# A one-core hybrid encoder layer: instructions placed by a model of the engines' timelines

## The chip, the core and the metric

The kernel runs on one core of a Trainium2 chip. The core has five engines that run their own instruction streams in order and meet only at semaphores: PE (TensorE, matmuls, with its weight loads shown apart as PEld), DVE (VectorE), ACT (ScalarE), POOL (GpSimd) and SP (SyncE, which here issues the DMAs). The metric is the device time of one execution in microseconds, lower is better.

## What is computed

One step of an encoder layer on 512 prompt frames and 64 sample frames, width 2048:

```python
mod = silu(c) @ w_ada + b_ada                       # 6 modulation vectors
h = rmsnorm(x, norm1) * (1 + sc1) + sh1
proj = h @ w_in                                     # q, k, v, gates of two mixers
o_a = gla(...)                                      # gated linear attention, 4 heads
o_b = gated_delta_rule(conv(q), conv(k), conv(v))   # 8 heads, needs a triangular inverse
x = x + g1 * (concat(o_a, o_b) @ w_out)
h = rmsnorm(x, norm2) * (1 + sc2) + sh2
x = x + g2 * (silu(causal_conv(h @ w_gate) + b) * (h @ w_val)) @ w_down
y = rmsnorm(x, final_norm)
```

The gated delta rule works in blocks. For one block it is, in short:

```python
lower = strict_tril((k * beta) @ k.T * decay)
sol = solve(eye + lower, [v * beta, k * beta * exp(G)])
u = sol_v - sol_k @ s
o = (q * exp(G)) @ s + (q @ k.T * decay) @ u
s = exp(G_last) * s + (k * exp(G_last - G)).T @ u
```

Both recurrences also return their states, and so do the two convolutions.

## The kernel before

Every product with a large weight is written as three float32r matmuls on split operands. A weight tile of 128 x 1024 is loaded by SP, ACT rounds it into a high part `wh` (L599) and DVE subtracts to get the low part `wl` (L600); PE then runs `wh` on the high and the low half of the activations (L512) and `wl` on the high half (L514). Three buffers each hold `raw`, `wh` and `wl`. The results lie in the two PSUM buffers named `g`. "Weight product" below means these L512 and L514 matmuls.

The stages stand in this order on PE. The head (0 to about 225 us of the profiled execution) loads x, transposes it (L645), makes the first modulation with matmuls at L672, and does the first products. Then the input projection runs tile by tile, while the recurrences are written as Python generators called jobs: after every six weight matmuls `tick` calls `job_step`, which advances the oldest job by one `yield`. It also advances the modulation blocks that DVE sums up (L772) and PE reduces (L778). The output projection of the second half of the heads follows, then that of the first half (about 1300 us), then the up projection as a seven-product scheme (L1300 to L1302, up to about 2400 us), then the down projection with the final norm (L1510).

The job of the gated delta rule (`gdn`, L155) runs once for each of the eight heads and a ninth time for the samples. Its steps on PE: transposes of k and q (L144, through `transpose4`), `kn.T kn` (L216), `kn.T q` (L222), then an inverse of the 16 x 16 diagonal blocks off PE (`inverse16`), then L238 and L244 twice with a transpose behind each pair, L253 and L258, the transposes of v, and four blocks of the recurrence itself, each of them a chain L276, L283, L289, with L303 and L305 for the output. Between any two of these stands a short operation of DVE or ACT that reads the PSUM bank and writes the next operand. At the end stands a norm (ACT squares, POOL power at L138, ACT scaling) and a transpose.

`inverse16` (L331) leaves PE altogether: the block goes to DRAM (L340), comes back transposed by four DMAs (L345), POOL runs 14 pairs of L351 and L352 on it, and it goes out and in again (L355, L358) before DVE spreads it (L362) for L238. `yield WAIT` and the numbers `REST_D` and `REST_X` make the job pass its turn some times while this runs.

What sets the order on each engine is the scheduler of the framework. It takes the instructions as traced, each with a priority (program order, moved forward by `high_priority(offset=80)` for the job's DVE and ACT operations and for the loading and splitting of weights), plays them on a model of the machine, and lays down for each engine the order in which they started there. Buffers limit it: the jobs and the gates of the linear attention (`gla_gate`, L1009) share 14 buffers `m` and 6 buffers `qkv`, and a tile that finds none free waits for a release.

## Time and profile before

| quantity | value |
|---|---|
| time, median of 3 runs | 2975.83 us (2970.51 to 2976.37) |
| profiled execution | 2988.47 us |
| its span, first to last instruction | 2986.8 us |
| PE busy | 2871.2 us (96%) |
| DVE busy | 2048.5 us (69%) |
| ACT busy | 1198.7 us (40%) |
| POOL busy | 334.5 us (11%) |
| HBM traffic | 131 GB/s over the span |
| mean granted clock of PE | 0.978 |

The profiled execution is 12.6 us longer than the median of the runs. In the page's slices PE is at nine tenths or more from the second tenth of the span on; in the windows that the prediction quotes it stands idle for a few per cent before 1300 us and hardly at all between 1300 and 2900 us. In those windows the columns are the busy time of each engine with its number of instructions, then the granted clock of PE (1.00 is full), the share of time in which the DMA engines were busy, and GB/s.

### The profile page before, as it was taken

The page shows a single profiled execution, that of the slowest core. Times are in us where ns is not written, and L with a number is a line of the kernel's source. Part 1 is how long each engine was busy: PE and PEld are TensorE (multiplying, and loading weights), DVE is VectorE, ACT ScalarE, POOL GpSimd, SP SyncE. Part 2 cuts the span into 40 slices and gives each one's busy share as a digit, 9 for nine tenths or more (in the row PEclk, how much of TensorE's full clock was granted, in tenths as well). Part 3 has the DMA queues.
Part 4 walks back from the last instruction along what each step waited for, and adds up shares of the span by engine and source line. Part 5 has one row for each costly group of instructions (what it writes and reads, how often), then busy time and mean ns, then how long its engine had stood idle before and what let it go on. Part 6 is the DMA issues. An engine that isn't in the chain of part 4 may idle for free.

```text
span 2986.8 us, 52415 instructions
## 1 busy us (share of the span) xinstructions
PE 2871.2 (96%) x21096; PEld 2774.8 (93%) x21096; DVE 2048.5 (69%) x3198; ACT 1198.7 (40%) x2062; POOL 334.5 (11%) x609
## 2 busy tenths in 40 slices
PE   6998899999899999999999999999999999999998
PEld 3688889999799998999999999999999999999997
DVE  2355776667568867557888888888888865555555
ACT  4235454444435433245444444444444421222223
POOL 0004342232210000000011011111101100000000
PEclk7999999999899999999999999999999999999999
DMA  8964554445454446743333333333333473333221
GB/s 251 286 191 118 143 161 130 129 129 147 123 156 131 140 128 184 201 141 97 111 104 105 113 100 106 113 104 104 114 106 104 133 235 101 111 101 115 86 80 65
DMA packets 535446, 395.55 MB, mean 132 GB/s; under 512 B 59657, under 2 KB 465412, under 8 KB 535204
## 3 DMA queue, kind: packets, MB, share of 16 engines
q1 hardware_dynamic: 535204, 392.21, 44.7%
q8 instruction: 166, 2.72, 0.4%
q14 instruction: 76, 0.62, 0.1%
HBM read 356.47 MB, written 35.67 MB: 131 GB/s over the span
## 4 chain that ended last, share of the span: by engine, by line
PE 80%; DVE 6%; DMA 4%; POOL 4%; ACT 3%; issue 2%; SPq 0%; ACTq 0%; POOLq 0%; DVEq 0%
PE g L512 25%; PE g L514 13%; PE bank L1301 11%; PE bank L1300 11%; PE bank L1302 11%; DVE acc L772 2%; DMA xr<-in_w_ada_dram 1%; PE bank L144 1%; PE bank L672 1%; POOL m L352 1%; POOL m L351 1%; POOL s L138 1%; PE bank L405 1%; PE bank L778 1%; ACT m L1623 1%
## 5 line engine op out<-in xcount | busy, mean ns | idle before, releaser
L1301 PE MATMUL bank<-slot,wh 128*128 128x290 f32 x2464 | 736.2, 299 | 0.0
L1300 PE MATMUL bank<-slot,wh 128*128 128x290 f32 x2464 | 733.9, 298 | 0.0
L1302 PE MATMUL bank<-slot,wl 128*128 128x290 f32 x2464 | 728.0, 295 | 0.0
L512 PE MATMUL g<-slot,wh 128*128 128x288 f32 x3168 | 551.6, 295 | 0.2 <-DVE slot L1070 0.2
L512 PE MATMUL g<-hh,wh 128*128 128x288 f32 x2048 | 470.0, 308 | 2.4 <-ACT wh L599 2.4
L1302 PEld LDWEIGHTS bank<-slot,wl 128*128 128x128 f32 x2464 | 470.6, 191 | 0.0
L1301 PEld LDWEIGHTS bank<-slot,wh 128*128 128x128 f32 x2464 | 469.7, 191 | 0.1
L512 PEld LDWEIGHTS g<-slot,wh 128*128 128x128 f32 x3168 | 465.8, 188 | 0.7 <-DVE slot L1070 0.5
L1300 PEld LDWEIGHTS bank<-slot,wh 128*128 128x128 f32 x2464 | 464.1, 188 | 0.1
L514 PE MATMUL g<-hh,wl 128*128 128x288 f32 x2048 | 461.9, 304 | 1.2 <-DVE wl L600 1.2
L599 ACT ACTIVATE wh<-raw 128x1024 fp32r<-128x1024 f32 x215 | 227.2, 1058 | 586.6 <-PE g L512 571.4
L512 PE MATMUL g<-hl,wh 128*128 128x288 f32 x2048 | 460.6, 304 | 0.0
L1070 DVE SCALAR_TENSOR_TENSOR slot<-g,mod,slot 128x512 f32<-128x512 f32 (+1 forms) x448 | 201.9, 491 | 287.9 <-PE g L514 286.3
L772 DVE SCALAR_TENSOR_TENSOR acc<-xr,ct,acc 128x512 f32<-128x512 f32 x480 | 341.5, 754 | 29.0 <-DMA xr<-in_w_ada_dram 28.1
L512 PEld LDWEIGHTS g<-hh,wh 128*128 128x128 f32 x2048 | 337.7, 193 | 14.7 <-issue 10.2
L514 PEld LDWEIGHTS g<-hh,wl 128*128 128x128 f32 x2048 | 338.9, 193 | 8.3 <-issue 6.0
L514 PE MATMUL g<-slot,wl 128*128 128x288 f32 x1584 | 342.8, 295 | 0.0
L512 PEld LDWEIGHTS g<-hl,wh 128*128 128x128 f32 x2048 | 338.9, 193 | 4.1 <-issue 3.7
L600 DVE TENSOR_TENSOR wl<-raw,wh 128x1024 fp32r<-128x1024 f32 x215 | 262.0, 1219 | 64.9 <-ACT wh L599 63.3
L1247 ACT ACTIVATE wh<-raw 128x1024 fp32r<-128x1024 f32 x176 | 186.0, 1057 | 222.6 <-PE bank L1301 194.2
L514 PEld LDWEIGHTS g<-slot,wl 128*128 128x128 f32 x1584 | 255.3, 188 | 0.0
L1248 DVE TENSOR_TENSOR wl<-raw,wh 128x1024 fp32r<-128x1024 f32 x176 | 215.4, 1224 | 54.0 <-ACT wh L1247 54.0
(346 smaller groups left out, 3180.4 us busy)
## 6 DMA issues: line engine op xcount, KB each, us to landing
raw<-in_w_up_dram SPq DMA_DIRECT2D x176, 512.0 KB
xr<-in_w_ada_dram SPq DMA_DIRECT2D x128, 512.0 KB
raw<-in_w_in_dram SPq DMA_DIRECT2D x100, 512.0 KB
raw<-in_w_down_dram SPq DMA_DIRECT2D x88, 512.0 KB
hraw<-in_w_ada_dram SPq DMA_DIRECT2D x64, 512.0 KB
raw<-in_w_out_dram SPq DMA_DIRECT2D x32, 512.0 KB
slot<-actd SPq DMA_DIRECT2D x44, 288.0 KB
actd<-v SPq DMA_DIRECT2D x44, 256.0 KB
```

Source lines behind the costliest of these rows:

```text
L138: self.nc.gpsimd.tensor_tensor(out[:parts, :n], out[:parts, :n], self.mhalf[:parts, :n], op=ALU.pow)
L512: T.matmul(ps[:, h if bank is None else bank, :n], wh, x[:, h, :n], start=f, stop=False)
L514: T.matmul(ps[:, h if bank is None else bank, :n], wl, ah[:, h, :n], start=False, stop=stop)
L599: nc.scalar.activation(hi[:, :n_], raw[:, :n_], AF.Copy)
L600: nc.vector.tensor_tensor(lo[:, :n_], raw[:, :n_], hi[:, :n_].bitcast(F32), op=ALU.subtract)
L772: V.scalar_tensor_tensor(acc[s], w[:, k], col, acc[s], op0=ALU.mult, op1=ALU.add)
L1070: self.nc.vector.scalar_tensor_tensor(x1[:, :, z], ps[:, :, c], gain[:, q:q + 1], x1[:, :, z], op0=ALU.mult, op1=ALU.add)
L1247: self.nc.scalar.activation(hi, src, AF.Copy)
L1248: self.nc.vector.tensor_tensor(lo, src, hi.bitcast(F32), op=ALU.subtract)
L1300: T.matmul(ps, wh[:, j], hi, start=(c < 3 and j == 0), stop=False, skip_group_check=True)
L1301: T.matmul(ps, wh[:, j], lo, start=False, stop=False, skip_group_check=True)
L1302: T.matmul(ps, wl[:, j], hi, start=False, stop=(j == NPAIR - 1), skip_group_check=True)
```

## The change

One argument is added where the context of the framework is opened. The traced instructions, their priorities, the tiles and the number of buffers stay as they are. What changes is the model on which the scheduler plays them: it keeps timelines for the engines in place of the plain one.

```diff
-    with tile.TileContext(nc) as tc:
+    with tile.TileContext(nc, schedule_with_timeline_sim=True) as tc:
         layer_kernel(tc, i, o)
```

Each engine has as many instructions as before (20165 on PE, 3200 on DVE, 1894 on ACT, 614 on POOL, 1138 on SP) in another order. From the up projection to the middle of the down projection the orders are nearly alike. They differ most between the third weight tile of the projections and the end of the recurrences. Three places on PE follow. The names in the rows: `g` is the output of a weight product, `bank` of any other matmul, `wh` and `wl` the weights, `hh` and `hl` the activations, `st`, `sq`, `m` and `qkv` the operands of a job.

The first is in the recurrence of the fourth head, at 518.9 us of the profiled execution. Before:

```order
L289 MATMUL bank_759_5241<-sq_758_5233,m_595_4109 128x128
L303 MATMUL bank_761_5245<-sq_758_5233,m_590_4077 128x128
L305 MATMUL bank_761_5245<-st_752_5206,qkv_561_3883 128x128
L512 MATMUL g_742_5163<-hl_206_1231,wh_767_5272 128x288
L276 MATMUL bank_762_5256<-st_760_5243,m_612_4266 128x128
L514 MATMUL g_742_5163<-hh_205_1230,wl_768_5273 128x288 x2
L512 MATMUL g_742_5163<-hh_244_1495,wh_767_5272 128x288 x2
L283 MATMUL bank_764_5266<-sq_763_5257,m_691_4768 128x128
```

The same step in the changed kernel:

```order
L305 MATMUL bank_761_5245<-st_752_5206,qkv_561_3883 128x128
L514 MATMUL g_1023_7039<-hh_152_915,wl_1026_7042 128x288 x2
L512 MATMUL g_1023_7039<-hh_191_1180,wh_1030_7115 128x288 x2
L512 MATMUL g_1023_7039<-hl_192_1181,wh_1030_7115 128x288 x2
L514 MATMUL g_1023_7039<-hh_191_1180,wl_1031_7116 128x288 x2
L512 MATMUL g_1023_7039<-hh_195_1192,wh_1030_7115 128x288 x2
L512 MATMUL g_1023_7039<-hl_196_1193,wh_1030_7115 128x288 x2
L514 MATMUL g_1023_7039<-hh_195_1192,wl_1031_7116 128x288 x2
L512 MATMUL g_1023_7039<-hh_200_1211,wh_1030_7115 128x288 x2
L512 MATMUL g_1023_7039<-hl_201_1212,wh_1030_7115 128x288 x2
L514 MATMUL g_1023_7039<-hh_200_1211,wl_1031_7116 128x288 x2
L276 MATMUL bank_762_5256<-st_760_5243,m_612_4266 128x128
```

Between L305 and L276 stood one weight matmul and now stand twenty, and they belong to a weight product that came several tiles later before (`g_1023` in place of `g_742`): the job runs later against the products.

The second is in the recurrence of the seventh head, at 745 us of the profiled execution. Before:

```order
L276 MATMUL bank_1109_7702<-st_1106_7688,m_964_6742 128x128
L512 MATMUL g_1096_7645<-hl_245_1496,wh_1121_7754 128x288 x2
L514 MATMUL g_1096_7645<-hh_244_1495,wl_1122_7755 128x288 x2
L512 MATMUL g_1096_7645<-hh_247_1506,wh_1121_7754 128x288 x2
L283 MATMUL bank_1111_7712<-sq_1110_7703,m_1043_7244 128x128
L512 MATMUL g_1096_7645<-hl_248_1507,wh_1121_7754 128x288 x2
L514 MATMUL g_1096_7645<-hh_247_1506,wl_1122_7755 128x288
L289 MATMUL bank_1113_7723<-sq_1112_7714,m_947_6585 128x128
L303 MATMUL bank_1115_7727<-sq_1112_7714,m_942_6553 128x128
```

The same steps in the changed kernel:

```order
L276 MATMUL bank_1109_7702<-st_1106_7688,m_964_6742 128x128
L283 MATMUL bank_1111_7712<-sq_1110_7703,m_1043_7244 128x128
L289 MATMUL bank_1113_7723<-sq_1112_7714,m_947_6585 128x128
L303 MATMUL bank_1115_7727<-sq_1112_7714,m_942_6553 128x128
L305 MATMUL bank_1115_7727<-st_1106_7688,qkv_915_6364 128x128
L276 MATMUL bank_1116_7738<-st_1114_7725,m_964_6742 128x128
L283 MATMUL bank_1118_7748<-sq_1117_7739,m_1043_7244 128x128
L289 MATMUL bank_1123_7765<-sq_1119_7750,m_947_6585 128x128
L303 MATMUL bank_1125_7769<-sq_1119_7750,m_942_6553 128x128
```

Here the weight matmuls between the links are gone: the weight tiles of the last head's projections stand ahead of this place now, and the next one (`g_1273`) comes 34 rows after this L276. From the middle of the sixth head's recurrence to that tile, 83 rows, there is no weight matmul at all.

The third is around the first L238 of the samples' recurrence, at 876 us. Before:

```order
L512 MATMUL g_1312_9062<-hh_94_581,wh_1314_9064 128x288 x2
L512 MATMUL g_1312_9062<-hl_95_582,wh_1314_9064 128x288 x2
L514 MATMUL g_1312_9062<-hh_94_581,wl_1315_9065 128x288 x2
L238 MATMUL bank_1317_9090<-m_1291_8919,m_1263_8658 128x64 x4
L512 MATMUL g_1312_9062<-hh_99_600,wh_1314_9064 128x288 x2
L512 MATMUL g_1312_9062<-hl_100_601,wh_1314_9064 128x288 x2
L514 MATMUL g_1312_9062<-hh_99_600,wl_1315_9065 128x288 x2
L512 MATMUL g_1312_9062<-hh_138_865,wh_1314_9064 128x288 x2
```

In the changed kernel:

```order
L1009 MATMUL bank_1307_9039<-na_1766,wg_1848 128x512
L1009 MATMUL bank_1308_9050<-na_1766,wg_1848 128x64
L238 MATMUL bank_1317_9090<-m_1291_8919,m_1263_8658 128x64 x4
L244 MATMUL bank_1318_9102<-m_1190_8232,m_1290_8918 128x64 x4
L144 MATMUL bank_1319_9115<-consts0_96,m_1291_8919 128x128 x4
L238 MATMUL bank_1320_9128<-m_1291_8919,m_1263_8658 128x64 x4
L244 MATMUL bank_1321_9140<-m_1190_8232,m_1290_8918 128x64 x4
L144 MATMUL bank_1323_9155<-consts0_96,qkv_1322_9153 128x128 x4
L276 MATMUL bank_1332_9185<-s0_1330_9181,m_1261_8640 64x128
L276 MATMUL bank_1332_9185<-s0_1331_9183,m_1261_8640 64x128
L283 MATMUL bank_1334_9196<-sq_1333_9186,m_1291_8919 128x128
L512 MATMUL g_1410_9579<-hh_85_550,wh_1412_9581 128x288 x2
```

Between this L238 and the L216 from which its inverse starts stood 130 rows before, most of them weight matmuls. Now stand there L222 x4, L144 x4, eight matmuls of L778 and the two of L1009, and no weight matmul.

## The prediction

> **What bounds the kernel now.** I read the page first: its span, the busy times, the slices and the chain.
>
> ```profile
> span 2986.8 us, 52415 instructions
> ...
> PE 2871.2 (96%) x21096; PEld 2774.8 (93%) x21096; DVE 2048.5 (69%) x3198; ACT 1198.7 (40%) x2062; POOL 334.5 (11%) x609
> ...
> PE   6998899999899999999999999999999999999998
> ...
> PEclk7999999999899999999999999999999999999999
> ...
> PE 80%; DVE 6%; DMA 4%; POOL 4%; ACT 3%; issue 2%; SPq 0%; ACTq 0%; POOLq 0%; DVEq 0%
> ```
>
> PE is the bound, and 80% of the chain is its own work. The order of instructions cannot make that work smaller; it can only change the time in which PE stands or runs at a lower clock. So the second view is the busy time by stage (us, busy PE, PEld, DVE, ACT, POOL with counts, clock, DMA share, GB/s):
>
> ```profile
> 0.00:225.00 225.00, 190.48 (x1225) 139.29 (x1226) 94.69 (x211) 73.53 (x130) 9.00 (x25) 0.92 0.79 242
> 225.00:660.00 435.00, 402.32 (x2977) 388.61 (x2976) 289.20 (x468) 219.31 (x559) 140.87 (x283) 0.95 0.49 136
> 660.00:925.00 265.00, 246.23 (x1817) 233.75 (x1815) 174.89 (x304) 118.49 (x289) 57.00 (x120) 0.95 0.50 141
> 925.00:1300.00 375.00, 361.76 (x2610) 345.89 (x2609) 265.58 (x485) 137.28 (x241) 11.13 (x25) 0.99 0.56 158
> 1300.00:1400.00 100.00, 100.00 (x759) 100.00 (x759) 69.15 (x126) 55.36 (x102) 4.81 (x17) 1.00 0.36 109
> 1400.00:2900.00 1500.00, 1497.41 (x11170) 1496.74 (x11169) 1105.18 (x1482) 567.61 (x677) 108.11 (x134) 1.00 0.38 112
> ```
>
> From 1300 to 2900 us PE loses 2.6 us in all and has its full clock; there the change can gain nothing, and the orders are nearly alike. At 759 matmuls in 100 us a weight matmul takes 0.132 us, which is my rate for work put between two job steps. What can be won lies ahead of 1300 us. I count loss as idle time plus (1 - clock) x length, an upper measure, since part of the low clock falls into idle time: 225 to 660 us loses 32.7 + 21.8 = 54, 660 to 925 us loses 18.8 + 13.3 = 32, 925 to 1300 us 13.2 + 3.8 = 17. The head loses 34.5 + 18 = 52, but there the DMA engines are 79% busy.
>
> What PE waits for in those stretches (who, releaser, us, times, longest; three stretches in turn):
>
> ```profile
> PE bank L144 <- ACT m L1623: 20.3, 7, 6.4
> PE bank L276 <- DVE st L1623: 6.1, 1, 6.1
> PE bank L144 <- ACT qkv L924: 3.9, 2, 2.4
> ...
> PE bank L144 <- ACT m L1623: 13.1, 6, 10.3
> PE bank L283 <- DVE m L1623: 2.5, 1, 2.5
> ...
> PE bank L144 <- DMA xr<-in_x_prompt_dram: 3.4, 4, 1.8
> PE bank L1224 <- DVE dg L1218: 2.6, 1, 2.6
> PE g L512 <- ACT wh L599: 2.4, 1, 2.4
> ```
>
> Almost all are links of the jobs: PE has come to a job's next matmul before ACT or DVE has made its operand. Weights are late once.
>
> **The change, stage by stage.** Nothing is added or removed; every job step is moved against the weight matmuls, on PE, DVE, ACT, POOL and SP alike, the DMAs of the inverse and the modulation with them.
>
> *225 to 660 us, the first heads.* What one step of the recurrence takes is in the instructions of PE and DVE in order of time:
>
> ```profile
> 517.00 0.49 PE L276 MATMUL bank<-st,m 128*128 128x128 f32 x2
> ...
> 518.00 0.49 PE L283 MATMUL bank<-sq,m 128*128 128x128 f32 x2
> ...
> 518.86 0.49 PE L289 MATMUL bank<-sq,m 128*128 128x128 f32 x2
> 519.18 0.39 PE L303 MATMUL bank<-sq,m 128*128 128x128 f32 x2
> 519.40 0.39 PE L305 MATMUL bank<-st,qkv 128*128 128x128 f32 x2
> ...
> 519.78 0.49 PE L276 MATMUL bank<-st,m 128*128 128x128 f32 x2
> ```
>
> A link takes 0.86 to 1.0 us and the step 2.78 us, of which the five job matmuls are 1.1 (five at 0.22, the distance from L303 to L305). Counted over the 36 links that end at L283, the middle one had 0.8 us of PE work to cover it and has 3.05 now, as the first place shown has: twenty weight matmuls, 2.6 us, where one stood. A link of 1 us is hidden then, with 2 us to spare for an ACT or DVE that is busy with something else. Waits of 6 us are not hidden whole. I leave 10 us of the idle time, from 3 (no link but the longest late) to 20 (the waits of L144 stay, since its cause is a queue and not the distance). The clock follows the waits:
>
> ```profile
> 386.00:393.00 7.00, 3.78 (x16) 3.77 (x17) 0.69 (x1) 1.97 (x5) 2.43 (x6) 0.55 0.61 138
> 567.00:574.00 7.00, 7.00 (x36) 7.00 (x35) 3.59 (x8) 3.98 (x20) 2.46 (x3) 0.54 0.71 208
> 642.00:649.00 7.00, 7.00 (x38) 6.98 (x36) 0.92 (x3) 3.89 (x19) 1.01 (x1) 0.55 0.29 76
> 758.00:772.00 14.00, 5.67 (x24) 5.66 (x25) 7.00 (x12) 1.97 (x5) 1.68 (x2) 0.53 0.68 186
> ...
> PE bank L144 <- ACT qkv L924: 1.5, 1, 1.5
> ```
>
> The last row is from the list of waits just ahead of the 642 us row: 1.5 us were enough for 7 us at about half clock with PE fully busy. So I take 8 of the 21.8 us as staying, with bounds 3 and 18. Gain: 54 - 18 = 36, between 54 - 38 = 16 and 54 - 6 = 48.
>
> [...]
>
> *660 to 925 us, the last heads.* The jobs now run later against the products, so the products come to their end with more than two heads' steps still to do, and the next tile waits for the buffers that those jobs hold. The second and third places shown are there. These stretches have the bare links:
>
> Of the L283 links 11 have under 0.6 us of cover now, where none had. I count 9 whole steps without cover: 9 x (2.78 - 1.1) = 15. Three norms at the end of a head now have their transpose right behind L305, with 0.14 us of work between. The link took this long before:
>
> ```profile
> 677.85 0.39 PE L305 MATMUL bank<-st,qkv 128*128 128x128 f32 x2
> ...
> 681.53 0.33 PE L144 MATMUL bank<-consts,m 128*128 128x128 f32 x1 [0.91 <-ACT m L1623]
> ```
>
> That is 3.7 us, so 3 x 3.7 = 11. The second half of the inverse, L238 to L258, without cover for the seventh head and half of it for the eighth and the samples: 10 links x 0.75 = 7. And the first half, off PE, at 839 us, of all engines in order of time, with the wait ahead of an instruction in brackets:
>
> ```profile
> 839.39 1.13 PE L216 MATMUL bank<-m 128*128 128x128 f32 x8
> ...
> 841.56 0.34 SPq L340 DMA_DIRECT2D d<-m  x1
> ...
> 845.85 1.40 SPq L345 DMA_DIRECT2D m<-d  x4
> ...
> 848.68 0.12 POOL L347 MEMSET m<- 32x16 f32 x1 [13.86 <-DMA m<-d]
> ...
> 860.59 0.32 SPq L355 DMA_DIRECT2D d<-m  x1
> ...
> 863.94 0.92 SPq L358 DMA_DIRECT2D cm<-d  x2
> ...
> 865.86 1.29 DVE L362 TENSOR_TENSOR m<-cm,consts 128x512 f32<-128x512 f32 x2 [6.06 <-DMA cm<-d]
> ```
>
> From L216 to the end of L362 pass 27.8 us. L238 needs that. In the samples' job the changed order puts 5 us of PE work between them (L222 and L144, eight of L778, two of L1009), so PE stands for 23. In the eighth head it puts 9 us, but the seventh head's recurrence and norm lie in between and wait for about 12 us of the terms above, so 7 are left. Sum 15 + 11 + 7 + 23 + 7 = 63, and 11 for clock and for waits that stay: 74 against 32 before, a loss of 42. Bounds: if a quarter of the links turn out covered and nothing else waits, 0.75 x 33 + 30 = 55, a loss of 23; if the low clock covers the whole stretch, with its 27 us of job matmuls at half rate, 101, a loss of 69.
>
> *925 to 1410 us.* The transposes of x (L144 and L1099) stand 4 to 6 us of PE work later against the products than before, which covers waits up to 1.8 us, and L1224 stands 3.2 us later, which covers its 2.6. The linear attention's links get 3 us as well; at some places a transpose or an eviction on ACT now stands close ahead of a product. With the low clock at the norm 23 us are lost there before; I leave 12. Gain 11, between 3 and 16.
>
> *Head and end.* In the head transposes and modulation matmuls change places, but the transfers that set it are the same: gain 3, between -5 and 6. The last transposes (L1510) stand closer behind their residuals, with 1.6 to 2.2 us of products between; the end is the same chain: 0.
>
> *Sum.* -36 + 42 - 11 - 3 = -8. The profiled execution took 2988.47 us, its span and 1.7 around it, so it would be 2980; the median of the runs is 12.6 below it, and 2975.8 - 8 = 2968.
>
> **Rivals.**
>
> *The stretch without products runs at half clock* (slower). Its place is between the sixth head's recurrence and `g_1273`, and the samples' inverse. The 758 us row speaks for it: 14 us at 0.53 with PE 40% busy. Against it: before that, in the same head, PE was dense with job matmuls and products mixed. Then the late stages lose 101 rather than 74, the sum is +19, and the time 2995. The change is slower from a late loss of 82 us on (32 + 36 + 11 + 3).
>
> *Both sides turn out at their good end* (faster). The early waits go with their clock (48), the late links have a quarter covered (+23), and the attention gains 16: -48 + 23 - 16 = -41, or 2935. For it speak the 3 us of cover; against it that 6 us waits came from DVE and ACT being held by other work, which the order does not cure.
>
> *The waits of the first heads stay* (slower). L144 waits for a chain through ACT and POOL which are as busy as before, and an eviction of `g` on ACT behind a job's operation can hold a product. The early gain is then 16 and the sum +12: 2988. Against it: the L276 and L283 links are simple, and their cover is three times what they take.
>
> **How the numbers follow.** The forecast has 0.45, half clock late 0.22, both good 0.20, waits that stay 0.13. From run to run the kernel before agrees to 0.2%, so 6 us on either side of 2975.8 are no difference. The forecast's own range is 2953 to 2984: 0.25 of it is faster, 0.14 the same, 0.06 slower. With both good, faster is 0.45; the same is 0.14 + 0.02 of the rest, 0.16; slower 0.39. The range goes from 2935, the good rival, to 3008, half clock late with 13 more, most of what the head (8) and the attention (8) can fall short.
>
> **What would show it.** Right: between 225 and 660 us a clock of 0.98 or more and PE idle for about 10 us; L238 in the list of PE's waits with one of about 20 us; a window of some 60 us with PE at half. Wrong: L144's waits for ACT unchanged in the first heads; L238 without a long wait, which would mean that the inverse starts earlier than L216's place says; a wait of a product for `wh`, `wl` or a bank of `g` among the longest.

## The result and the profile after

The changed kernel takes 3096.91 us (median of 4 runs, 3093.65 to 3097.89), the kernel before 2976.10 us in the same set (4 runs, 2970.51 to 2980.33). The ratio is 1.0396, with a 95% interval of 1.038 to 1.0413: 121 us slower. The forecast was 2968, its range ended at 3008.

The page of the changed kernel, its span, busy times, slices of PE and of the clock:

```profile
span 3095.1 us, 52436 instructions
...
PE 2891.1 (93%) x21096; PEld 2810.2 (91%) x21096; DVE 2046.5 (66%) x3198; ACT 1199.5 (39%) x2062; POOL 296.5 (10%) x609
...
PE   6999999988595899899999999999999999999998
...
PEclk8999999998586899899999999999999999999999
```

The hole lies between the ninth and the fourteenth slice, about 600 to 1070 us. Before it, the slices are fuller than they were.

To see where the time went, the two kernels must be compared at the same work, not at the same time. I gave each matmul the median distance from one start to the next that its line has in the trace of before, and summed that along PE's order: "PE work". The time at which a place is reached, less the PE work ahead of it, is what has been lost so far. Idle time is what the records show between matmuls; the rest of a loss is matmuls that ran slowly (in the head it comes out negative, since the median distances hold some idle time of their own). The head's figures hang on the price given to the L672 matmuls, whose starts come in bunches; the other stages hardly move with it.

| PE work, us | before: lost (idle + slow) | changed: lost (idle + slow) | forecast difference | measured |
|---|---|---|---|---|
| 0 to 200, head | 29.0 (30.7 - 1.7) | 20.0 (34.0 - 13.9) | -3 | -9 |
| 200 to 550, first heads | 59.1 (32.7 + 26.4) | 25.0 (13.7 + 11.2) | -36 | -34 |
| 550 to 800, last heads | 40.1 (18.8 + 21.4) | 166.4 (106.9 + 59.4) | +42 | +126 |
| 800 to 1100, linear attention | 31.8 (13.2 + 18.5) | 55.7 (26.7 + 29.0) | -11 | +24 |
| 1100 to 2600 | 5.9 | 10.7 | 0 | +5 |

The sum is +112; the spans differ by 108. The same stages as windows, first of before, then of the changed kernel (length, busy PE, PEld, DVE, ACT, POOL with counts, clock, DMA share, GB/s):

```profile
232.00:642.00 410.00, 377.32 (x2800) 364.32 (x2799) 277.15 (x446) 204.97 (x515) 136.59 (x277) 0.96 0.50 139
642.00:932.00 290.00, 271.23 (x1996) 258.04 (x1995) 186.62 (x334) 129.57 (x321) 59.54 (x123) 0.95 0.47 131
932.00:1263.00 331.00, 317.76 (x2285) 302.82 (x2284) 243.08 (x445) 121.07 (x215) 11.13 (x25) 0.99 0.57 162
```

```profile
225.00:598.00 373.00, 359.27 (x2740) 356.57 (x2740) 222.63 (x347) 168.32 (x403) 108.86 (x233) 0.97 0.45 128
598.00:1015.00 417.00, 310.07 (x2028) 291.90 (x2027) 220.96 (x381) 157.16 (x416) 80.12 (x167) 0.77 0.40 116
1015.00:1370.00 355.00, 328.28 (x2296) 313.82 (x2294) 257.85 (x491) 126.93 (x227) 10.02 (x25) 0.93 0.51 147
```

About the same number of matmuls took 373 us in place of 410, then 417 in place of 290, then 355 in place of 331. What PE waited for in the middle stretch of the changed kernel (who, releaser, us, times, longest):

```profile
PE bank L144 <- ACT m L1623: 37.8, 4, 11.9
PE bank L238 <- DVE m L362: 30.0, 1, 30.0
PE bank L283 <- DVE sq L1623: 10.3, 9, 2.6
PE bank L289 <- ACT sq L1623: 6.3, 11, 1.0
PE bank L144 <- DVE m L1623: 5.6, 3, 3.2
PE bank L276 <- DVE st L1623: 5.4, 4, 2.1
```

The 30.0 of L238 is the samples' inverse, for which I had 23. The 37.8 are four norms, at the ends of the fourth to the seventh head, 8 to 12 us each; I had three, at 3.7. The last of them, from the end of the seventh head's recurrence to its transpose, in order of time:

```profile
838.12 0.63 PE L305 MATMUL bank<-st,qkv 128*128 128x128 f32 x2
...
839.40 0.19 ACT L1623 ACTIVATION_READ_ACCUMULATOR sq<-m 128x1 f32 x1
...
842.14 0.75 DVE L772 SCALAR_TENSOR_TENSOR acc<-xr,ct,acc 128x512 f32<-128x512 f32 x1 [4.96 <-DMA xr<-in_w_ada_dram]
842.88 0.69 DVE L362 TENSOR_TENSOR m<-cm,consts 128x512 f32<-128x512 f32 x1
843.49 0.74 DVE L772 SCALAR_TENSOR_TENSOR acc<-xr,ct,acc 128x512 f32<-128x512 f32 x1
844.15 0.68 DVE L362 TENSOR_TENSOR m<-cm,consts 128x512 f32<-128x512 f32 x1
844.75 0.34 DVE L1623 SCALAR_TENSOR_TENSOR st<-st,egl,bank 128x128 f32<-128x128 f32 x1
845.01 1.41 DVE L772 SCALAR_TENSOR_TENSOR acc<-xr,ct,acc 128x512 f32<-128x512 f32 x2
...
846.34 0.16 DVE L137 TENSOR_SCALAR s<-s 128x4 f32<-128x4 f32 x1
846.58 1.01 POOL L138 TENSOR_TENSOR s<-s,mhalf 128x4 f32<-128x4 f32 x1 [8.67 <-DVE s L137]
847.62 1.28 ACT L1623 ACTIVATE m<-m,s 128x128 f32<-128x128 f32 x4 [8.03 <-POOL s L138]
848.07 0.18 PEld L144 LDWEIGHTS bank<-consts,m 128*128 128x128 f32 x1 [9.62 <-ACT m L1623]
```

ACT has the sums of squares at 839.6. L137, which needs nothing else, starts at 846.3. In between DVE stands for 5 us in front of a sum of the modulation (L772), whose transfer has not landed, and then does four sums and three other operations that stand ahead of L137 in its order. The norm, and PE behind it, wait for a transfer that has nothing to do with them. The list of waits names ACT, two steps from the cause.

In the other three norms ACT itself is the larger part. The longest, at the end of the fourth head:

```profile
614.07 0.63 PE L305 MATMUL bank<-st,qkv 128*128 128x128 f32 x2
614.48 1.28 ACT L1623 ACT_TABLE_LOAD   x1
...
616.95 1.28 ACT L924 ACT_TABLE_LOAD   x1
...
618.89 1.28 ACT L1623 ACT_TABLE_LOAD   x1
...
623.57 0.19 ACT L1623 ACTIVATION_READ_ACCUMULATOR sq<-m 128x1 f32 x1
624.30 0.16 DVE L137 TENSOR_SCALAR s<-s 128x4 f32<-128x4 f32 x1
...
626.60 0.48 PE L144 MATMUL bank<-consts,m 128*128 128x128 f32 x1 [11.90 <-ACT m L1623]
```

Here the squares are ready only at 623.8 us, since ACT does operations of the heads to come and three table loads of 1.28 us between them; the step to DVE adds 0.5 us. At the ends of the fourth, fifth and sixth head the squares are ready 9.7, 9.7 and 5.7 us after L305 starts, at the seventh 1.5 us, and in the kernel before 1.2 or 1.3 us at every head.

### The profile page after: what moved, and what is told of

Its sections match the earlier page's. It is cut to its first block, busy times and chain, and to the rows that moved or that the text cites. A ratio compares the mean times of both kernels' runs of the same rounds, so it can differ in the third digit from the quotient of the medians.

```text
span 3095.1 us, 52436 instructions
## 1 busy us (share of the span) xinstructions
PE 2891.1 (93%) x21096; PEld 2810.2 (91%) x21096; DVE 2046.5 (66%) x3198; ACT 1199.5 (39%) x2062; POOL 296.5 (10%) x609
## 4 chain that ended last, share of the span: by engine, by line
PE 60%; DMA 2%; DVE 1%; ACT 0%; issue 0%; POOL 0%; ACTq 0%; SPq 0%; DVEq 0%; POOLq 0%
PE g L512 18%; PE bank L1301 11%; PE bank L1300 11%; PE bank L1302 10%; PE g L514 9%; DMA xr<-in_w_ada_dram 1%; DMA xr<-in_x_prompt_dram 0%; PE bank L1510 0%; DVE acc L772 0%; PE bank L144 0%; PE bank L405 0%; DVE slot L1152 0%; DMA slot<-xd 0%; PE bank L778 0%; POOL slot L1134 0%
## 5 line engine op out<-in xcount | busy, mean ns | idle before, releaser
L1302 PE MATMUL bank<-slot,wl 128*128 128x290 f32 x2464 | 714.8, 296 | 0.6 <-DVE wl L1248 0.6
L512 PE MATMUL g<-hh,wh 128*128 128x288 f32 x2048 | 461.2, 305 | 4.9 <-ACT ts L1049 1.9
L772 DVE SCALAR_TENSOR_TENSOR acc<-xr,ct,acc 128x512 f32<-128x512 f32 x480 | 338.7, 751 | 65.0 <-DMA xr<-in_w_ada_dram 64.9
L600 DVE TENSOR_TENSOR wl<-raw,wh 128x1024 fp32r<-128x1024 f32 x215 | 262.7, 1222 | 108.7 <-ACT wh L599 107.0
```

The source lines that it names most:

```text
L512: T.matmul(ps[:, h if bank is None else bank, :n], wh, x[:, h, :n], start=f, stop=False)
L600: nc.vector.tensor_tensor(lo[:, :n_], raw[:, :n_], hi[:, :n_].bitcast(F32), op=ALU.subtract)
L772: V.scalar_tensor_tensor(acc[s], w[:, k], col, acc[s], op0=ALU.mult, op1=ALU.add)
L1302: T.matmul(ps, wl[:, j], hi, start=False, stop=(j == NPAIR - 1), skip_group_check=True)
```

## The experiments

The time of the kernel before in the sets below was 2981.83 (first four), 2982.51 (next four), 2982.86 (next four) and 2980.63 us (last). Single runs are given as such. The losses by stage, worked out as above:

| kernel | us | head | first heads | last heads | attention |
|---|---|---|---|---|---|
| before (profiled 2988.47) | 2976.10 | 29 | 59 | 40 | 32 |
| changed | 3096.91 | 20 | 25 | 166 | 56 |
| e1 at most 8 steps behind | 3040.66 | 22 | 88 | 53 | 48 |
| e2 at most 32 steps behind | 3038.14 | 24 | 31 | 95 | 59 |
| e3 changed, short inverse | 3069.82 | 20 | 11 | 153 | 56 |
| e4 before, short inverse | 2938.15 | 29 | 29 | 23 | 30 |
| e5 timeline, PE of before | 3099.00 | 29 | 98 | 78 | 60 |
| e6 plain, PE of changed | 3160.26 | 33 | 63 | 190 | 44 |
| e7 before, inverse on DVE | 2960.15 | 27 | 44 | 26 | 37 |
| e8 from 32 steps to 8 | 3068.63 | 24 | 98 | 72 | 44 |
| e9 timeline, PE and DVE of before | 2997.03 | 29 | 72 | 31 | 36 |
| e10 timeline, PE and ACT of before | 3096.20 | 33 | 100 | 67 | 66 |
| e11 changed, few sums | 3031.57 | 25 | 24 | 121 | 32 |
| e12 before, few sums | 2964.41 | 31 | 49 | 23 | 33 |

**e1 and e2: how far the jobs may fall behind.** `mm6` is put under the framework's rule that its matmuls come on PE after a given instruction, here the last matmul of the job step traced `LAG` steps earlier:

```diff
+LAG = 8            # 32 in e2
...
-            self.job_step()
+            self.paced_step()      # notes the step's last PE instruction in self.steps
...
-    def mm6(self, ps, wh, wl, act, start, stop, halves=((0, HT), (1, HT)), bank=None):
+    def mm6(self, *a, **kw):
+        with self.paced():
+            self.mm6_now(*a, **kw)
...
+def _paced(self):
+    steps = getattr(self, "steps", [])
+    if not getattr(self, "jobs", None) or len(steps) <= LAG:
+        return nullcontext()
+    return self.tc.issue_after(steps[-1 - LAG])
```

> The changed kernel with one rule added: a weight matmul may not be placed on PE ahead of the last matmul of the job step that was traced eight job steps before it. So the jobs can't fall further behind the products than eight steps; the timeline model still sets the rest, DVE, ACT, POOL and SP among it. Theory 'lag' (the late loss comes from PE's products running ahead until the buffers stop them, which leaves 27 and 10 us of job matmuls bare): the gain of the first heads stays (about 40 us against before), the late loss goes, no stretch at half clock and no L238 wait over 10 us: 2920 to 2955 us. Theory 'other queues' (the timeline model's order on DVE and ACT puts the convolutions and the modulation's sums ahead of the jobs' links, and that is what PE waits for): the waits of L144 for ACT stay at 40 us or more, the time stays above 3040 us.

> The same rule with 32 job steps in place of eight. In this order 10 us of job matmuls stand bare after the seventh head and 10 us in the samples' inverse, against 27 and 10 in the changed kernel. Theory 'lag': the loss follows the bare stretch, so the time lies between the eight-step kernel and the changed one: 2990 to 3050 us, with the L238 wait of some 25 to 30 us still there, since only 4.3 us of PE work stand between L216 and L238 as in the changed kernel. Theory 'other queues': no different from the changed kernel, 3080 us or more.

Eight steps: 3040.66 us (3038.12 to 3045.88, 4 runs), ratio 1.0201, interval 1.0172 to 1.023. That is far above the range of "lag" and just on the bound of "other queues" (above 3040), whose other sign is missing: L144 waits 21.3 us for ACT, not 40 or more. The stages say why. The loss in the last heads fell from 166 to 53 us, close to the 40 of before: that part of "lag" held. But the first heads lost 88 in place of 25. With the products bound to the jobs, PE met the jobs' late links there:

```profile
PE bank L144 <- ACT m L1623: 21.2, 4, 19.5
PE bank L144 <- DVE m L1623: 17.3, 9, 4.1
PE bank L144 <- ACT qkv L924: 9.3, 2, 7.7
```

This is the list of waits of e1 from 225 to 664 us. Its PE order is near that of before (a matmul stands 8 rows away on the average, of 20165), and yet these three rows come to 47.8 us, where the same three had 25.2 in the kernel before (20.3, 1.0 and 3.9). The one wait of 19.5 us is a matter of SP: ACT stands there for a transfer of `gd` (L170) that SP issues at 264.7 us, right behind the last transfers of the inverse (L355 at 262.1, L358 at 263.8). So the links themselves have become slower with the changed kernel's orders on the other engines, and its products, running ahead, hid it in the first heads. Thirty-two steps, 3038.14 us (one run, expected 2990 to 3050): 31 us lost in the first heads and 95 in the last, with the L238 wait of 30.3 us still there. In the last heads the loss follows the bare stretch, as "lag" says; the whole time does not lie between the eight-step kernel and the changed one, as it had, since the first heads lose little here.

**e3 and e4: what the inverse costs.**

```diff
             for i in range(1, 15):
...
-            G.tensor_tensor(xt[:, rest, :i], ..., op=ALU.mult)
-            G.tensor_tensor(xx[:, rest, :i], ..., op=ALU.add)
+            if i == 1:
+                G.tensor_tensor(xt[:, rest, :i], ..., op=ALU.mult)
+                G.tensor_tensor(xx[:, rest, :i], ..., op=ALU.add)
```

> The changed kernel with one of the 14 pairs of L351 and L352 left, the other 13 left out (the inverse of the 16 x 16 blocks is not computed). The bare stretches of PE's order stay. If the samples' first inverse is exposed as I read it, L238's wait of 30 us shrinks by the pairs' time, about 11 us, to about 19, and the time falls by 11 to 16 us, to about 3083. If the wait is made by the transfers of the inverse alone or by something else ahead of L362 on DVE, wait and time stay within 4 us.

> The kernel before with the same 13 pairs left out. There the inverse has 35 to 53 us of PE work to hide behind, so nothing is won: 2968 to 2982 us. If it falls by more than 8 us, the inverse was on the path before too, and my price of its exposure in the changed kernel is too high by that.

The changed kernel took 3069.82 us (one run), 27 less; L238's wait went from 30.0 to 15.6. So the inverse is bare there, and 14 us of the 27 are that wait. I had expected 11 to 16 us in all; the rest came mostly in the first heads, which lost 11 in place of 25. The kernel before took 2938.15 us (one run), 44 less than before in the same set. That miss is a find: in the kernel before no L238 waited for the inverse, and leaving its pairs out still won 44 us. The order of time before one of the L144 waits of 6.4 us, in the trace of before, shows how:

```profile
381.08 0.19 ACT L1623 ACTIVATION_READ_ACCUMULATOR sq<-m 128x1 f32 x1
...
381.62 0.27 DVE L137 TENSOR_SCALAR s<-s 128x4 f32<-128x4 f32 x1
...
384.12 1.14 POOL L352 TENSOR_TENSOR m<-m 32x44 f32<-32x44 f32 x1
...
387.15 0.59 POOL L354 COPY m<-m 32x256 f32<-32x256 f32 x1
387.72 1.01 POOL L138 TENSOR_TENSOR s<-s,mhalf 128x4 f32<-128x4 f32 x1
...
388.76 1.28 ACT L1623 ACTIVATE m<-m,s 128x128 f32<-128x128 f32 x4 [6.55 <-POOL s L138]
389.22 0.18 PEld L144 LDWEIGHTS bank<-consts,m 128*128 128x128 f32 x1 [6.66 <-ACT m L1623]
```

L137 has its result at 381.9; L138 starts at 387.7, since POOL is in the middle of the next head's run of pairs. The norm of one head waits in POOL's queue behind the inverse of the next.

**e7: the inverse off POOL.**

```diff
-            G.tensor_tensor(xt[:, rest, :i], ..., op=ALU.mult)
-            G.tensor_tensor(xx[:, rest, :i], ..., op=ALU.add)
+            nc.vector.tensor_tensor(xt[:, rest, :i], ..., op=ALU.mult)
+            nc.vector.tensor_tensor(xx[:, rest, :i], ..., op=ALU.add)
```

> The kernel before with the 14 pairs of the inverse on DVE in place of POOL; nothing is left out. Leaving 13 of the pairs out won 44 us, though no L238 waited: POOL's 12 us run of pairs stands ahead of a norm's L138, and PE waits for that norm. If POOL's queue is the cause, the pairs on DVE win most of it, less what 28 short operations cost in DVE's queue (about 4 us a head, mostly beside other work): 2940 to 2962 us, with L144's waits for ACT under 15 us. If it is the inverse's own length that counts, or DVE is as full as POOL, 2970 to 2995 us.

2960.15 us (2956.34 to 2961.16, 4 runs), ratio to before 0.9918, interval 0.9896 to 0.994. It is the fastest kernel of this study that leaves nothing out. The waits of PE from 225 to 700 us, where L144 had waited 21.2 us for ACT in the kernel before:

```profile
PE bank L144 <- ACT m L1623: 11.2, 8, 3.4
PE g L514 <- DVE wl L600: 6.1, 1, 6.1
```

The L144 waits are halved, and a weight split on DVE is late once instead. Half of the 44 us comes back; the other half is what the pairs cost in DVE's queue, or what stays in POOL's; these runs do not part the two.

**e5 and e6: PE's order of the one, the rest of the other.** All matmuls are chained in a given order by a list of instruction numbers; the model then places the other engines round them.

```diff
-        layer_kernel(tc, i, o)
+        layer_kernel(tc, i, o); _pin(tc)
...
+def _pin(tc):                       # ORDER: the numbers of PE's instructions, in the other kernel's order
...
+    ins = {x.name: x for x in tc.nc.cur_bb.bb.instructions}
+    for ids in json.loads(zlib.decompress(base64.b85decode(ORDER))).values():
+        last = None
+        for n in ids:
+            x = ins.get(f"I-{n}")
...
+            if last is not None:
+                tc.add_manual_dep(x, last.name, mybir.DependencyInfo(mybir.DependencyClass.NoSync, mybir.DependencyReason.DATA),
+                                  reason="issue_after")
+            last = x
```

> The timeline model stays on, but PE's 20165 instructions are held to the order of the kernel before; DVE, ACT, POOL and SP are placed by the timeline model round them. Theory 'PE order': the whole difference comes from where the job matmuls stand against the products, so the kernel goes like the one before: 2965 to 2990 us, and from 550 to 800 us of PE work about 40 us are lost, as before, where the changed kernel loses 166. Theory 'other queues': the timeline's order on ACT, DVE and POOL costs by itself, so 3010 us or more.

> The mirror image: the plain model, with PE held to the changed kernel's order. Theory 'PE order': 3080 to 3110 us, with an L238 wait of about 30 us and a clock of 0.5 to 0.8 from 700 to 900 us. Theory 'other queues': the plain placing of ACT and DVE gives the links faster, the waits of L144 for ACT fall from 46 us to under 20, and the time is 3050 us or less.

The timeline model with PE's order of before: 3099.00 us (one run), as slow as the changed kernel, though every matmul stands in the order of the kernel before. "PE order" as the whole cause falls. The loss lies elsewhere than in the changed kernel, 98 in the first heads and 78 in the last. The shares of the chain that ended last, from 233 to 681 us of e5, and under it from 232 to 642 us of before:

```profile
by line: DVE acc L772 14.6%; PE g L512 11.5%; issue 7.5%; ACT m L1623 5.7%; PE g L514 5.5%; DMA xr<-in_w_ada_dram 5.2%; POOL m L352 4.9%; DVE wl L600 4.9%; POOL m L351 4.6%; DVE ca L922 4.3%; DMA d<-m 4.0%; PE bank L144 3.3%; DMA m<-gd 2.7%
```

```profile
by line: PE g L512 18.7%; PE g L514 9.4%; POOL m L352 7.2%; POOL m L351 6.7%; DVE acc L772 5.8%; issue 5.6%; ACT m L1623 4.5%; DMA xr<-in_w_ada_dram 4.4%; PE bank L144 4.2%; DVE ca L922 3.0%; POOL s L138 3.0%; DMA d<-m 2.5%; PE bank L778 1.
```

The sums of the modulation went from 5.8% of the chain to 14.6%. In e5's DVE order the jobs' operations (L1623) stand 4.6 places later than before on the average, up to 21, and L772 4.0 earlier. That is little beside PE's order, where the change moves some matmuls by hundreds of rows, and I had not looked at it.

The mirror image, plain with the changed kernel's PE order, took 3160.26 us (one run), outside both theories: three products wait 18 to 23 us for `ts` of L965 on ACT, 64 us in all, a place where a foreign PE order and the plain order of ACT do not fit. But its bare stretch, from 676 to 710 us of PE work, loses 67 us against 71 in the changed kernel, and L238 waits 25.0. That part belongs to PE's order whichever model places the rest. The norms do not: L144 waits 14.3 us for ACT in the last heads there, where the changed kernel waits 37.8, and the squares are ready 1.2 to 1.9 us after L305 starts. Their length comes from the order that the timeline model gives to the other engines.

**e9 and e10: DVE or ACT held as well.** The list of e5 with DVE's instructions added, or ACT's.

> The timeline model, with PE and DVE held to the order of the kernel before; ACT, POOL and SP are placed by the timeline model. With PE alone held so, the time was 3099 us. In that kernel's DVE order the jobs' own operations (L1623) stand 4.6 places later on the average, up to 21, and the modulation's sums (L772) 4.0 earlier. Theory 'DVE order': that is what made the links late, so the time comes back to 2975 to 3010 us. Theory 'ACT or SP order': DVE's places are not it, 3070 us or more.

> The same with PE and ACT held to the order of the kernel before, DVE left to the timeline model. Theory 'DVE order': little is won, 3070 to 3105 us. Theory 'ACT order' (the longest waits with PE alone held were L144 for ACT, 53 us): 2975 to 3030 us.

With DVE held the time came back to 2997.03 us, with ACT held it stayed at 3096.20 (one run each). So of the 116 us by which e5 is behind the kernel before, 102 go with DVE's order. The last 14 are not settled; ACT, POOL and SP differ by about one place on the average there. What ACT's order costs with PE in the changed kernel's order, where the squares come late, was not run.

**e11 and e12: the sums taken away.**

```diff
-                    else:
+                    elif k0 == 0:
                         V.scalar_tensor_tensor(acc[s], w[:, k], col, acc[s], op0=ALU.mult, op1=ALU.add)   # L772
```

> The changed kernel with 448 of the 480 sums of L772 left out (the modulation is summed over two of 128 rows' blocks only; its transfers stay). Theory 'DVE order': the changed kernel suffers from job operations that stand behind sums of 0.75 us and behind the transfers that these wait for, so it wins much more than the kernel before does from the same cut: the distance between the two falls from 120 us to 70 or less, and what stays is the bare stretch. Theory 'bare stretch alone': both win the same 20 to 40 us, and the distance stays at 100 us or more, this one at 3050 us or more.

> The kernel before with the same 448 sums left out. In its chain from 232 to 642 us the sums have 5.8% and the transfers for them 4.4%, 42 us; some of that would be taken by the next late thing (POOL's pairs have 14%). So 20 to 40 us are won: 2940 to 2962 us, by both theories.

(Left out are 448 of the 480 sums: each block is summed over two of its sixteen groups of rows.) The changed kernel fell to 3031.57 us, by 65, the kernel before to 2964.41, by 18 (one run each). The distance between them is 67 us where it was 121, as "DVE order" had it. The attention's loss, 56 in the changed kernel, is 32 without the sums, which is what it was before the change. The last heads still lose 121 against 23. The kernel before won a little less than the 20 to 40 expected. L238's wait stays and the norms shrink:

```profile
PE bank L238 <- DVE m L362: 30.3, 1, 30.3
PE bank L144 <- ACT m L1623: 21.9, 5, 6.8
```

These are the waits of e11 from 0 to 1400 us; L144 had 46.0 in the whole of the changed kernel. That L238's wait is the same is chance. POOL's pairs for the samples take 9.3 us in e11 (901.7 to 911.0) in place of 16.7 (944.5 to 961.2), but the next transfer of the inverse, L355, is issued by SP only at 916.7 us, behind five loads of modulation rows.

**e8: both bounds in turn.** `LAG` goes from 32 to 8 over 192 job steps (`max(8, 32 - n // 8)`).

> The changed kernel with the bound on how far the jobs may fall behind going from 32 job steps at the start to 8 after 192 steps. If lag helps in the first heads (it covers POOL's run of pairs) and harms in the last ones (the products are gone), both at once give the good ends: 30 us lost from 200 to 550 us of PE work (32 steps lost 31, 8 steps 88), 53 from 550 to 800 (8 steps lost 53, 32 steps 95), the rest as in those two, so 2970 to 2990 us. If the two bounds' waits are not of that kind, the time stays at 3020 us or more, as with 8 and with 32.

3068.63 us (one run): worse than either bound alone. The first heads lost 98 where 32 steps throughout lost 31, and L144 waited 33.7 us for ACT there. This bound tightened while the links were slow, and PE waited for them. With e1 and e2 the miss says that the lag in the first heads was not a fault of the new order; it was what hid the slow links.

**e13: the clock in the bare stretch.** Still open was why 59 us of the late loss are slow matmuls and not idle time.

```diff
-                rhs = r
+                rhs = r; fill(ps, u[:, b], kn)      # behind L276; the same behind L283 and L305
...
+def _filler(self, n):
...
+        if n in (6, 7):                             # seventh and eighth head
+            self.nc.tensor.matmul(ps[:, 256:512], w, x.rearrange("p b t -> p (b t)")[:, :256], start=True, stop=True)
```

> The changed kernel with a matmul of 128x256 added right behind each L276, L283 and L305 group in the recurrences of the seventh and eighth head, 22 in all, into an unused part of the same bank; nothing reads them. At full clock one takes about 0.43 us (twice the 0.22 of a 128x128), 9.5 us in all, and the operand that the next link waits for takes 0.9 to 1 us, so most of it lies in PE's idle time. Theory 'gaps set the clock': in the seventh head's recurrence, where PE was busy 37% of the time at a clock of 0.52, the clock rises above 0.7, and the time stays the same or falls, 3080 to 3100 us. Theory 'low clock whatever fills the gaps': the clock stays under 0.6 there, the added matmuls run at half rate (0.8 us each, 18 in all) and the time rises to 3105 us or more.

3093.05 us (one run): no slower, with 22 matmuls more. The seventh head's recurrence in the changed kernel, and under it with the matmuls added:

```profile
820.00:849.00 29.00, 10.64 (x34) 7.58 (x34) 19.06 (x34) 4.71 (x18) 14.78 (x31) 0.52 0.49 139
```

```profile
820.00:850.00 30.00, 13.83 (x53) 9.38 (x53) 18.76 (x34) 4.74 (x19) 15.76 (x31) 0.73 0.49 139
```

PE is busier and its clock is 0.73 in place of 0.52, as "gaps set the clock" had it. But the stretch is no shorter for it (30 us in place of 29), so the run shows that the clock rises there when matmuls stand in the gaps, and not how much of the 59 us the low clock costs.

## Why the prediction was wrong

- *First heads, gain 36 (16 to 48).* Measured 34. The clock there is 0.97 and PE idle for 13.7 us, where I had written 0.98 and 10. Size and place were right. The reason was right only in half: I held that longer distances would cover links as they had been. They covered links that had become slower; without the distance the same stage lost 88 to 100 us (e1, e5, e8, e10). That the number fits is therefore in part luck.
- *Last heads, loss 42 (23 to 69).* Measured 126. This is the step that failed, in four of its terms. "Three norms at 3.7, 11": four norms, 37.8 us. L238 of the samples, 23: 30.0. The other bare links, 15 + 7 + 7 = 29: the rest of the 106.9 idle, 39. Clock and others, 11: 59 us of slow matmuls. The places were nearly all as foretold, from the order alone; the durations were not. I took each link's time from the trace of before and kept it, as if DVE and ACT would serve it as they had. The norm of the seventh head shows the difference on DVE, 6.7 us between the squares and L137, that of the fourth head the difference on ACT. The samples' inverse was longer too, mostly on POOL: from L347 to the next transfer (L355) pass 17.5 us (944.4 to 961.9) in place of 11.9. And 3.7 us was one norm of nine in the kernel before: from L305 to the transpose seven took 3.0 to 4.9 us, but two took 9.2 and 12.8. In the longest, which is the wait of 10.3 us in the prediction's own list, the squares were ready at 754.7 us and L137 started at 764.2: the wait in DVE's queue was already there to be read. The signs that I named for being right (a long wait of L238, a stretch at half clock) told of places, so they came true without testing the durations.
- *The clock, 11.* I had the row of 758 us, 14 us at 0.53, and gave its consequence to a rival with 0.22, priced at 27 us more. This rival was nearest: the stretch without products ran at a clock of 0.67 to 0.52, from 765 to 870 us. But even its late loss was 101.
- *Attention, gain 11 (3 to 16).* Measured a loss of 24. With the sums left out the stage loses 32 us in the changed kernel and 33 in the kernel before (e11, e12), so the whole loss of 24 goes with the sums on DVE, and the longer distances won about nothing without them. Nothing in the prediction stands for it: of DVE I had asked only what its operations wait for, not what stands ahead of them.
- *Head, gain 3; end, 0.* Measured a gain of 9 in the head. From 1100 to 2600 us of PE work 5 us were lost, and the end after that won the 4 us by which the table's sum and the spans differ.
- *"Both good end" and "waits of the first heads stay".* Neither happened. The waits of the second are seen in another kernel: with PE held to before's order (e5) they stay and grow, and the stage loses 98 us in place of 59.
- *Nothing is added or removed.* True, and it led me to weigh only PE's order, since PE bounds the kernel. The change moved every queue, and with PE held it was DVE's queue that decided 102 of 116 us.

What the runs leave is this account. The timeline model puts DVE's work in an order in which the jobs' short operations stand behind the modulation's sums and the transfers that these wait for; that slows the jobs' links (e5, e9, e11). At three of the four long norms ACT's order puts the next head's operations ahead of the squares; that is read from the trace and from e6, and was not tried by itself. On PE it lets products pass the late jobs. In the first heads this hides the slow links and wins 34 us; at the end the products are used up and the links are bare (e1, e2, e6), in the changed kernel at a clock of 0.67 to 0.52 from 765 to 870 us. Why the model judges so was not tried.

## What to carry to other kernels

Read a new order on every in-order queue that feeds the bound engine, not on the bound engine alone: here about five places on DVE were worth 102 us. A duration that is taken from the old trace holds only if what stands ahead of the operation in its queue is the same (the norm taken at 3.7 us had PE waiting 8 to 12 us here); count the work ahead of each link, and the transfer that this work waits for, and look at the longest case in the old trace as well as at a typical one. When a wait's releaser is idle or has other work, follow the chain back another step: the list said ACT, and at some norms the cause was DVE's queue, at one POOL's, and at three ACT's own.

## What the runs showed of the hardware

The figures of this section are from the traces and run times of this case. From 800 to 817.7 us of the changed kernel the clock was at half, though PE had only short gaps. Four stretches of its trace:

```profile
807.00:814.00 7.00, 6.66 (x35) 6.57 (x36) 2.33 (x7) 1.76 (x5) 0.00 (x0) 0.50 0.01 4
...
817.70:821.20 3.50, 1.16 (x6) 0.78 (x6) 3.50 (x8) 1.16 (x5) 0.00 (x0) 0.99 0.54 147
...
828.00:835.00 7.00, 3.50 (x12) 2.35 (x10) 6.40 (x12) 0.65 (x2) 6.14 (x12) 0.50 0.50 150
...
870.00:877.00 7.00, 7.00 (x56) 7.00 (x55) 6.24 (x11) 1.06 (x1) 0.00 (x0) 1.00 0.56 160
```

In the first PE is busy for 6.66 of 7 us and still at 0.50; from 800 to 819 us no gap was longer than 0.61 us. The records are longer at the lower clock (an L276 pair takes 0.79 us at 821.3, at half clock, and 0.49 at 517.0 in the kernel before, at full clock), so a busy share in such a row says little. The clock fell at 773.4 us, came back for 3.4 us at 817.7 (the second row), fell again at 821.2, and came back at 868.9, 5.4 us after the start of the first weight product behind the bare stretch (863.5). The matmuls of the first row are transposes, products of 64x64, sums of one column and, from 812.5 us, products of 128x128 (L216); whether their kind or the short gaps held the clock down was not tried.

In the traces of before and of the changed kernel 42 of the 44 stretches below full clock last a whole multiple of 3.4 us (from 3.4 to 47.8), and the other two are cut off by the end of the kernel. In the kernel before, a wait of 1.5 us (L144, up to 640.9) is followed by 6.8 us at half clock, from 642.7 to 649.5.

In the changed kernel the clock fell during a gap of 2.6 us (from 771.2; the clock fell at 773.4) and one of 2.0 us (from 819.3; at 821.2), and then stayed at half for 44.4 and 47.8 us.

The second find is the 44 us that the kernel before wins when 13 of the inverse's 14 pairs are left out (e4), though no matmul that uses the inverse waited for it. About 22 of them come back when the pairs move from POOL to DVE (e7).

On POOL the operations of one form differ much from one to the next: L352 on 32x54 took 0.29 us at 377.10 and 1.17 us at 852.39 in the trace of before. In the run of pairs at 848.7 us 26 of the 28 operations took 0.20 to 0.30 us; the two others, of 1.17 and 1.07 us, began while DVE made a split (L600, at 852.16 and 858.55). In the two traces every L351 or L352 during which DVE stood idle, 133 in the kernel before and 146 in the changed one, took 0.20 to 0.30 us. Those of over 0.6 us, 42 and 53, all ran beside an instruction of DVE, though 70 and 40 others did so in 0.35 us or less. The samples' whole run of pairs took 16.7 us in the changed kernel, where DVE does twenty sums beside it, and 9.3 us in e11, where 448 of the 480 sums are left out. Why POOL's operations took longer beside DVE's was not tried.
